# Experts from the seventh on in an order counted on chip, the two fullest with two blocks on one set of panels

## The chip, the cores and the metric

The kernel runs on one core of a Trainium2 chip. The metric is the device time of one execution in microseconds; smaller is better. It is one program: a first transformer block, a second block's mixer, and a mixture of experts (MoE) at the end. The change touches the MoE alone, the last 330 us or so.

## The reference, cut to what matters

```python
T = 512; D_MODEL = 1024; N_EXPERTS = 32; TOP_K = 2; D_EXPERT = 256

def hierarchical_moe(h, w_group, b_group, w_router, b_router, w_gate, w_up, w_down):
    ...
    grp = jnp.argmax(grp_probs, axis=-1)              # one of 4 groups of 8 experts
    top_p, top_e = lax.top_k(jax.nn.softmax(in_grp, axis=-1), TOP_K)
    weights = p_grp[:, None] * top_p / jnp.sum(top_p, axis=-1, keepdims=True)
    expert_id = grp[:, None] * EXPERTS_PER_GROUP + top_e
    ...
    def run_block(args):
        xb, e, wb = args
        a = jax.nn.silu(xb @ w_gate[e]) * (xb @ w_up[e])
        return (a @ w_down[e]) * wb[:, None]
    ...
    y = jnp.zeros((T, D), h.dtype).at[slot_tok].add(out.reshape(cap, D))

# second_block, after its mixer:
#     x = x + gate2 * hierarchical_moe(modulate(rms_norm(x)), ...);  return rms_norm(x, final_norm_g)
```

All is float32. Each of 512 tokens goes to two experts, 1024 assignments in all. An expert has three weight panels (gate, up, down) of 1024 x 256 floats, 1.05 MB each. Routing is a function of the inputs: counted from the reference, the experts 0 to 31 get

25 7 19 47 22 11 27 40 | 8 80 59 5 32 11 29 34 | 16 32 40 34 14 35 30 15 | 55 89 56 43 12 41 48 8

tokens. Two of them are over 64: expert 9 with 80 and expert 25 with 89.

## The kernel before, in words

A unit of MoE work is a `Pair` (a job): two blocks of up to CAP = 64 tokens, side by side on the 128 partitions. Each block is multiplied with its own expert's panels, as two matmuls that each fill 64 columns of the array (`both`, L1887). Pair c holds experts 2c and 2c+1. Tokens past the 64th of an expert go to a seventeenth job, number NP = 16, whose two blocks (SX = 2) belong to whichever experts overflow; its six panels come by indirect DMAs on GpSimd (L1680) through a table `xi`. `ORDER` (L31) puts that job thirteenth. If there were more than SX such blocks, a conditional part (L1407) would run eight further jobs and the final norm again.

The loop over jobs (L1372) does for job i: transpose the activations `a` of job i-1 (`turn_a`: PE L212, ACT copy `aT` L1910); transpose the gathered tokens of job i+1 (`turn`, L1877); start the gather of job i+2 from `h2d` in DRAM (L1865, POOL queue); gate and up products (`up`: 32 matmul calls, 64 rows in the profile since a float32 matmul runs in two passes; then Silu L1900 on ACT and the scaling L1901 on DVE); and the down product of job i-1 (`product`, 16 rows), scaled on DVE (L1919) into `o`. A scheduler then orders the instructions on each engine, so `down` may come before or after the next `up`.

The result of a job goes one of two ways:

- **Scattered**: `o` is written by an indirect DMA to `ye` in DRAM (L1933), one row of 4 KB for each valid token. Near the end `results` (L1471) clears a tile, gathers the two rows of each token from `ye` (L1476), and DVE adds them to `x` (L1392).
- **Hot**: `o` is split into two float32r halves `k` (L198) and spread onto `x` by one-hot matmuls (`spread`, L1956, 8 steps of two, each step with one DVE addition L1964 that frees its PSUM bank). `HOT` lists eight pairs. In order of execution these are jobs 4, 6, 8, 10 and 13 to 16; the spreads of the last two belong in part to `tail`.

Panels land in 17 places that are used in turn (`place`, L1663). SP issues one DMA for each panel (L1676), in order, and before each it waits until PE is done with the panel 17 places earlier. Panels of job 0 start while the second block's last products run. The router (`route`, L1479) counts each token's position within its expert by matmuls, builds the table of gathers `tab` and of scatters `to`, and leaves the rest of the tables and the weights `ws` to `rest` (L1583), which DVE computes while job 0 starts.

Of the kernel before, what the change touches and what calls it, by code (L numbers as in the profile page):

```python
# [9 lines left out]
F32 = mybir.dt.float32  # L10
# [8 lines left out]
P = 128  # L19
# [41 lines left out]
def shape_constants():  # L61
# [27 lines left out]
        it(8) * P + i[:, None] - float(2 * T), np.broadcast_to(np.repeat([float(c not in HOT) for c in range(NP)], 2).astype(f), (P, 32)),  # L89
        it(NX), i[:, None] + 0.0 * it(1), (it(XT) + 1.0) * CAP,  # L90
# [8 lines left out]
class Emit:  # L99
# [1151 lines left out]
    def route_loads(self, mod, op):  # L1251
# [7 lines left out]
        widths = (4, 8, 32, P, 8, 32, NX, 1, XT)  # L1259
# [76 lines left out]
    def moe(self):  # L1336
# [3 lines left out]
        with ExitStack() as c0:  # L1340
# [3 lines left out]
            tab, to = (rp.tile([P, NP + NX // 2], I32, tag=n, name=n) for n in ("tab", "to"))  # L1344
            src = rp.tile([P, 2, 8], I32, tag="src", name="src")
# [133 lines left out]
    def route(self, r1, rp, tab, to, src, W, xb, nx, sc, kept, ws):  # L1479
        nc, I = self.nc, self.I  # L1480
        d4, d8, i32, iP, tokv, away, jx, ip, thr = self.rt
# [43 lines left out]
        m1 = first_max(ing, d8, 8, h12[:, 0])  # L1525
        ing2 = tl(NT, 8)
        V.scalar_tensor_tensor(ing2, h12[:, 0], -BIG, ing, op0=ALU.mult, op1=ALU.add)
        m2 = first_max(ing2, d8, 8, h12[:, 1])
# [36 lines left out]
        vm = tl(8, 32, dt=F32R)  # L1565
        tt_(vm, flat(E), bc(tokv, 32), ALU.mult)
# [6 lines left out]
        rows, last = table(vm, 32, slice(0, NP))  # L1573
# [4 lines left out]
        with self.tc.issue_after(last.ins):  # L1578
            V.tensor_copy(to[:, 0:NP], rows)
            V.tensor_copy(kept, tab[:, 0:NP])  # L1580
            V.tensor_copy(cum, b[:, 0:160])

        def rest(room, room2):  # L1583
            tl = carve(room)

            cnt = cum[:, 128:160]
            n5 = tl(32, XT)
            tt_(n5, bc(cnt, XT), row(thr, 32), ALU.is_gt)
            V.tensor_reduce(nx, n5, axis=AX.X, op=ALU.add)
            z = tl(32)  # L1590
            V.memset(z, 0.0)
# [3 lines left out]
            for o, v in ((ei, row(away, 8)), (xi, row(xb, 8))):  # L1595
                tt_(flat(t), flat(E), v, ALU.mult)
                V.tensor_reduce(o, flat(t), axis=AX.X, op=ALU.add)
# [3 lines left out]
            V.tensor_scalar(ov, pos, float(CAP), None, op0=ALU.is_ge)  # L1601
            V.scalar_tensor_tensor(c, bl, -float(CAP), pos, op0=ALU.mult, op1=ALU.add)

            tt_(xi, xi, bl, ALU.add)
            tt_(xi, xi, ov, ALU.mult)
            eq = tl(8, NX)
            tt_(eq, row(jx, 8), bc(xi, NX), ALU.subtract)
            V.tensor_scalar(eq, eq, -1.0, None, op0=ALU.is_equal)
            tt_(vx, eq, bc(tokv, NX), ALU.mult)
            tt_(oc, row(iC, 8), bc(c, CAP), ALU.is_equal)  # L1610
            rows, _ = table(vx, NX, slice(NP, None), "d")
            V.tensor_copy(to[:, NP:], rows)


            m, f = tl(8), tl(8)
            V.scalar_tensor_tensor(m, pos, float(CAP), ei, op0=ALU.is_lt, op1=ALU.mult)
            V.scalar_tensor_tensor(f, xi, SX + 0.5, ov, op0=ALU.is_le, op1=ALU.mult)
            tt_(m, m, f, ALU.add)
            tt_(f, ov, f, ALU.subtract)
            for i, v in enumerate((m, f)):  # L1620
# [3 lines left out]

            tl2 = carve(room2)
# [11 lines left out]

            ge, gs, ex, s1 = tl(NT, 4), tl(NT), tl(NT), tl(NT)
            tt_(ge, gl, bc(gm, 4), ALU.subtract)
            tt_(ex, m2, m1, ALU.subtract)  # L1640
            nc.scalar.activation(ge, ge, AF.Exp)
            nc.scalar.activation(ex, ex, AF.Exp)
            V.tensor_reduce(gs, ge, axis=AX.X, op=ALU.add)
            V.reciprocal(gs, gs)
            V.tensor_scalar(s1, ex, 1.0, None, op0=ALU.add)
            V.reciprocal(s1, s1)
            tt_(W[:, 0, :], gs, s1, ALU.mult)
            tt_(W[:, 1, :], W[:, 0, :], ex, ALU.mult)
# [21 lines left out]

    def panel_of(self, which, e):
# [3 lines left out]
        if e < 32:  # L1675
            nc.sync.dma_start(raw, w[e].rearrange("(p k) c -> p (k c)", p=P))  # L1676
        else:
            if e >= 32 + SX:
                nc.vector.memset(raw, 0.0)
# [6 lines left out]
def PANELS(c):  # L1686

    return [(w, 2 * c + s) for w in ("gate", "up") for s in range(2)] + [("down", 2 * c + s) for s in range(2)]
# [163 lines left out]
class Pair:  # L1852
# [50 lines left out]
    def turn_a(self):  # L1903
# [5 lines left out]
        self.aT = self.tl("aT", 2, P)  # L1909
# [11 lines left out]
    def down(self, kept=None):  # L1921
        em = self.em
        if kept is not None and self.c in HOT:
# [13 lines left out]
    def hot(self, kept):  # L1937
        em, nc = self.em, self.nc
        self.o = self.tl("o", D)
        if self.c in ORDER[-2:]:  # L1940
# [47 lines left out]
```

## Time and profile before

| | |
|---|---|
| median of 3 runs | 1559.29 us (1558.46 to 1559.35) |
| the profiled execution: its own time | 1565.86 us |
| span of its profile | 1564.1 us |
| PE busy, DVE, ACT, POOL | 1483.3 us (95%), 908.5 (58%), 581.0 (37%), 206.3 (13%) |
| bytes read from and written to HBM | 259.91 MB and 19.44 MB, 179 GB/s over the span |
| DMA rate in four of the last ten of 40 slices | 425, 425, 425 and 420 GB/s |

Time in the profile counts from the span's start. Matmuls are pipelined and their ends are modelled, so a busy PE is not PE at its peak; the distance between two starts tells more than one duration. The granted clock is TensorE's, 1.00 for 2.4 GHz and 0.50 for 1.2 GHz; a number between them is a mean over a stretch with some of each.

### The profile page before, as it was taken

To read this page: it belongs to the slowest core of one execution; us is meant where nothing else is said; L and a number is where in the kernel's file an instruction comes from. 1 tells how busy PE (TensorE), PEld (TensorE's weight loads), DVE (VectorE), ACT (ScalarE), POOL (GpSimd) and SP (SyncE) were. 2 spreads that over 40 slices of the span, in tenths; PEclk is the share of its full clock that TensorE was granted. 3 is DMA by queue.
4 is the path that set the end of the run, shared out by engine and by line. 5 is a ranking of instruction groups with operands and counts; after the bars stand their busy time and mean duration, and the time that the engine had idled before them with its cause. 6 is when DMAs were issued, how large, how long until landed. Compare 5 with 4: busy or idle time off the path is not lost.

```text
span 1564.1 us, 20461 instructions
## 1 busy us (share of the span) xinstructions
PE 1483.3 (95%) x7742; PEld 1159.7 (74%) x7742; DVE 908.5 (58%) x1934; ACT 581.0 (37%) x1227; POOL 206.3 (13%) x235
## 2 busy tenths in 40 slices
PE   7999899999999999999999999999999789998885
PEld 6877778787888888887888888888887655455542
DVE  5675787877676765468766352248855641433162
ACT  4444675743232323345444342236632211111012
POOL 2110131101011010030000010000022211012310
PEclk8999999999999999999999999999999989999998
DMA  5325103057656654333322333421167679999941
GB/s 187 106 65 181 65 28 95 1 155 261 204 163 214 201 176 135 123 135 100 118 82 54 96 113 124 141 94 55 39 224 286 258 313 401 425 425 425 420 192 56
DMA packets 133056, 271.09 MB, mean 173 GB/s; under 512 B 19237, under 2 KB 78662, under 8 KB 119897
## 3 DMA queue, kind: packets, MB, share of 16 engines
q1 hardware_dynamic: 119834, 241.87, 43.1%
q0 software_dynamic: 9664, 25.04, 4.3%
q10 hardware_dynamic: 3454, 2.82, 0.6%
q8 instruction: 63, 1.03, 0.3%
q14 instruction: 41, 0.33, 0.1%
HBM read 259.91 MB, written 19.44 MB: 179 GB/s over the span
## 4 chain that ended last, share of the span: by engine, by line
PE 66%; DMA 10%; DVE 6%; issue 5%; ACT 2%; POOL 2%; SPq 0%; ACTq 0%; DVEq 0%; POOLq 0%
PE b L152 18%; PE b L153 18%; PE b L151 18%; PE b L1887 4%; PE b L212 3%; DMA pw<-w_expert_gate 2%; DMA pw<-w_expert_down 2%; DMA pw<-w_expert_up 1%; DMA ye<-o,to 1%; DVE wl L145 1%; PE b L1956 1%; PE b L816 1%; DMA xg<-h2d,tab 1%; DMA pw<-ye,src 1%; PE b L817 1%
## 5 line engine op out<-in xcount | busy, mean ns | idle before, releaser
L145 DVE TENSOR_TENSOR wl<-wr,wh 128x512 fp32r<-128x512 f32 x349 | 237.4, 717 | 144.1 <-ACT wh L143 132.5
L143 ACT ACTIVATE wh<-wr 128x512 fp32r<-128x512 f32 x361 | 205.3, 622 | 305.8 <-PE b L152 146.6
L1887 PE MATMUL b<-pw,xT 128*64 128x256 f32 x1088 | 133.3, 385 | 1.5 <-DMA pw<-w_expert_gate,xi 1.5
L151 PE MATMUL b<-h2h,wh 128*128 128x512 f32 (+1 forms) x320 | 122.6, 384 | 0.0
L152 PE MATMUL b<-h2l,wh 128*128 128x512 f32 (+1 forms) x320 | 122.4, 383 | 0.0
L153 PE MATMUL b<-h2h,wl 128*128 128x512 f32 (+1 forms) x320 | 122.3, 382 | 0.0
L1887 PEld LDWEIGHTS b<-pw,xT 128*64 128x64 f32 x1088 | 82.9, 138 | 46.2 <-issue 10.6
L152 PE MATMUL b<-fl,wh 128*128 128x512 f32 (+1 forms) x288 | 105.3, 366 | 0.0
L151 PE MATMUL b<-fh,wh 128*128 128x512 f32 (+1 forms) x288 | 105.0, 367 | 0.2 <-ACT fh L197 0.2
L153 PE MATMUL b<-fh,wl 128*128 128x512 f32 (+1 forms) x288 | 105.2, 366 | 0.0
L152 PE MATMUL b<-wl,uh 128*128 128x512 f32 x256 | 99.9, 390 | 0.2 <-DVE wl L145 0.2
L151 PE MATMUL b<-wh,uh 128*128 128x512 f32 x256 | 100.1, 391 | 0.0
L153 PE MATMUL b<-wh,ul 128*128 128x512 f32 x256 | 99.8, 390 | 0.0
L492 DVE SCALAR_TENSOR_TENSOR acc<-wr,cond,acc 128x512 f32<-128x512 f32 x84 | 62.9, 749 | 38.7 <-DMA wr<-mod_w 37.0
L153 PEld LDWEIGHTS b<-h2h,wl 128*128 128x128 f32 x320 | 61.0, 190 | 11.5
L152 PEld LDWEIGHTS b<-h2l,wh 128*128 128x128 f32 x320 | 61.0, 190 | 11.3
L151 PEld LDWEIGHTS b<-h2h,wh 128*128 128x128 f32 x320 | 60.8, 191 | 11.3
L1887 PE MATMUL b<-pw,aT 128*64 128x512 f32 x272 | 67.5, 600 | 0.5 <-ACT aT L1910 0.5
L151 PEld LDWEIGHTS b<-fh,wh 128*128 128x128 f32 x288 | 54.1, 189 | 9.6 <-ACT fh L197 0.5
L152 PEld LDWEIGHTS b<-fl,wh 128*128 128x128 f32 x288 | 54.4, 189 | 8.9 <-DVE fl L198 0.2
L153 PEld LDWEIGHTS b<-fh,wl 128*128 128x128 f32 x288 | 54.4, 189 | 8.8
L151 PEld LDWEIGHTS b<-wh,uh 128*128 128x128 f32 x256 | 48.1, 188 | 11.1 <-issue 1.4
(586 smaller groups left out, 3288.9 us busy)
## 6 DMA issues: line engine op xcount, KB each, us to landing
wr<-w_in SPq DMA_DIRECT2D x33, 1024.0 KB
pw<-w_expert_gate SPq DMA_DIRECT2D x32, 1024.0 KB
pw<-w_expert_up SPq DMA_DIRECT2D x32, 1024.0 KB
pw<-w_expert_down SPq DMA_DIRECT2D x32, 1024.0 KB
wr<-mod_w SPq DMA_DIRECT2D x24, 1024.0 KB
wr<-w_up SPq DMA_DIRECT2D x16, 1024.0 KB
wr<-w_down SPq DMA_DIRECT2D x16, 1024.0 KB
wr<-w_cmp SPq DMA_DIRECT2D x4, 1024.0 KB
```

Of the source, the lines that this page charges most:

```text
L143: nc.scalar.activation(hi[:, c], raw[:, c], AF.Copy)
L145: (nc.gpsimd if i in pool else eng or nc.vector).tensor_tensor(lo[:, c], raw[:, c], hi.bitcast(F32)[:, c], op=ALU.subtract)
L151: mm(o, lh, rh, start=first, stop=False)
L152: mm(o, lh, rl, start=False, stop=False)
L153: mm(o, ll, rh, start=False, stop=last)
L212: self.nc.tensor.transpose(o, i, self.ident[:k, :k])
L492: nc.vector.scalar_tensor_tensor(acc, rv[:, k, :], self.cond[:, kk:kk + 1], acc, op0=ALU.mult, op1=ALU.add)
L816: nc.tensor.matmul(o, v, ph, start=kind == 2, stop=False)
L817: nc.tensor.matmul(o, v, pl, start=False, stop=kind == 1 and kb == qb)
L1887: self.nc.tensor.matmul(o[h, :], x[:, k, h], w[s](k), start=k == ks[0], stop=k == ks[-1])
L1956: self.nc.tensor.matmul(b, self.oh[:, tt * P:(tt + 1) * P], k[:, half * 512:half * 512 + 512], start=first and i == 0, stop=last and i == 1)
```

## The change

There are still 17 jobs. The first three are pairs 0 to 2 with experts 0 to 5 (SE = 6), as before. DVE then finds the two fullest of experts 6 to 31; they become jobs 3 and 4, and each has one set of three panels on which both of its blocks run (up to 128 tokens of one expert). The remaining 24 experts, in their old order, make jobs 5 to 16. Which expert that is, is data: DVE writes a list `eid`, SP loads an entry into a register (`expert`, L1705 of the changed kernel), and the DMA of a panel takes its address from the register. The overflow job is gone, and with it the six indirect panels; more than one extra block for a fullest expert, or any for another, leads to the conditional part. Hot are jobs 13 to 16 only; all others are scattered. The additions of gathered rows to `x` are pinned to the place that the program gives them. `aT` has one buffer instead of two.

```diff
-NP = 16
+SE = 6
+ND = 32 - SE
+NP = 17
+NB = 2 * NP
 NX = 16
-SX = 2
-HOT = (4, 6, 8, 10, 12, 13, 14, 15)
-ORDER = [*range(12), NP, *range(12, NP)]
+HOT = 13
...
+            self.eid = rp.tile([P, ND], I32, tag="eid", name="eid")
...
-                jobs = [Pair(self, ep, XG[i % XGS], tab, to, c) for i, c in enumerate(ORDER)]
+                jobs = [Pair(self, ep, XG[i % XGS], tab, to, i) for i in range(NP)]
...
-                hot = lambda i: i >= 0 and jobs[i].c in HOT
-                back = max(i for i in range(n) if not hot(i)) + 2
+                hot = lambda i: i >= HOT
+                back = HOT + 1
...
-                            nc.vector.tensor_tensor(x[:, tt, :], y[:, k, :], x[:, tt, :], op=ALU.add)
+                            self.pin(nc.vector.tensor_tensor(x[:, tt, :], y[:, k, :], x[:, tt, :], op=ALU.add))
...
-                with self.tc.If(more > SX):
-                    for c in range(NP + SX // 2, NP + NX // 2):
+                with self.tc.If(more > 0):
+                    for c in range(NP, NP + NX // 2):
...
-        rows, last = table(vm, 32, slice(0, NP))
+        rows, last = table(vm, SE, slice(0, SE // 2))
...
         def rest(room, room2):
...
+            V.scalar_tensor_tensor(key, cnt, 32.0, ko, op0=ALU.mult, op1=ALU.add)
+            V.tensor_reduce(m1, key, axis=AX.X, op=ALU.max)
+            V.tensor_scalar(o1, key, m1, None, op0=ALU.is_equal)
+            V.scalar_tensor_tensor(key, o1, -1e6, key, op0=ALU.mult, op1=ALU.add)
+            V.tensor_reduce(m2, key, axis=AX.X, op=ALU.max)
+            V.tensor_scalar(o2, key, m2, None, op0=ALU.is_equal)
...
+            V.tensor_copy(ids[:, 0:1], m1)
+            V.tensor_copy(ids[:, 1:2], m2)
+            V.tensor_copy(self.eid, ids)
...
+            rows, _ = table(vx, NB + NX - SE, slice(SE // 2, None), "d")
...
+    def expert(self, e):
+
+        return self.nc.values_load(self.eid[0:1, e - SE:e - SE + 1], engines=(mybir.EngineType.SP,), min_val=0, max_val=31,
+                                   skip_runtime_bounds_check_because="the numbers of the experts from SE to 31, by their counts")
+
     def panel_of(self, which, e):
...
-        if e < 32:
-            nc.sync.dma_start(raw, w[e].rearrange("(p k) c -> p (k c)", p=P))
+        if e < SE:
+            nc.sync.dma_start(raw, whole(w[e]))
+        elif e < 32:
+            nc.sync.dma_start(raw, whole(w[bass.ds(self.who[e], 1)].rearrange("o r c -> (o r) c")))
...
+def EXPERTS(c):
+    two = (SE // 2, SE // 2 + 1)
+    if c in two:
+        return [SE + two.index(c)]
+    return [2 * c + s - (2 if c > two[1] else 0) for s in range(2)]
...
         if self.panels is None:
+            em.who = {e: em.expert(e) for e in EXPERTS(self.c) if SE <= e < 32}
             self.panels = [em.panel_of(*w) for w in PANELS(self.c)]
+        if len(self.panels) == 3:
+            self.panels = [p for p in self.panels for _ in range(2)]
...
-        self.aT = self.tl("aT", 2, P)
+        self.aT = self.tl("aT", 2, P, bufs=1)
```

How the change moves instructions shows at three places. On SP, where the panels of job 2 end and those of job 3 begin (`pw` is a panel's place, `eid` the list of experts), there stood before:

```order
L1676 DMA pw_11180<-w_expert_down 128x2048
L1676 DMA pw_11182<-w_expert_down 128x2048
L1676 DMA pw_11258<-w_expert_gate 128x2048
L1676 DMA pw_11260<-w_expert_gate 128x2048
L1676 DMA pw_11262<-w_expert_up 128x2048
```

and now:

```order
L1716 DMA pw_11204<-w_expert_down 128x2048
L1716 DMA pw_11206<-w_expert_down 128x2048
L1707 TENSOR_LOAD eid
L1718 ISA
L1718 DMA pw_11285<-w_expert_gate 128x2048
L1718 ISA
L1718 DMA pw_11287<-w_expert_up 128x2048
L1718 ISA
L1718 DMA pw_11289<-w_expert_down 128x2048
L1707 TENSOR_LOAD eid
```

Job 3 has three panels for six, each expert has one load of its number, and each panel one more instruction (ISA, two multiplications of registers) ahead of its DMA.

On PE, in the middle of the MoE, before the change: from the end of the down product of job 8 (`aT`) to the gate product (`xT`) of job 9, with the first steps of a spread (`k`, `oh`).

```order
L1887 MATMUL b_11919<-pw_11744,aT_11836 64x512
L1887 MATMUL b_11919<-pw_11746,aT_11836 64x512
L1956 MATMUL b_11963<-k_11904,oh_11906 128x512
L1956 MATMUL b_11971<-k_11904,oh_11906 128x512
L1887 MATMUL b_11866<-pw_11854,xT_11720 64x256
L1956 MATMUL b_11963<-k_11905,oh_11906 128x512
L1956 MATMUL b_11971<-k_11905,oh_11906 128x512
L1956 MATMUL b_11979<-k_11904,oh_11906 128x512
L1956 MATMUL b_11979<-k_11905,oh_11906 128x512
```

In the changed kernel no row of a spread stands on PE before job 13's down product. 32 such rows are left ahead of the tail's, where there were 96.

On DVE, near the end, before the change: the split and the additions of gathered rows (L1392, `pw`), around the activations `a` of job 14.

```order
L1919 TENSOR_TENSOR o_12443<-b_12451,S_10015 128x512
L198 TENSOR_TENSOR k_12445<-o_12443,k_12444 128x512
L1392 TENSOR_TENSOR x_10012<-pw_12428,x_10012 128x1024
L1919 TENSOR_TENSOR o_12443<-b_12459,S_10015 128x512
L1392 TENSOR_TENSOR x_10012<-pw_12428,x_10012 128x1024
L198 TENSOR_TENSOR k_12445<-o_12443,k_12444 128x512
L1901 SCALAR_TENSOR_TENSOR a_12424<-b_12407,ws,a_12424 128x256
```

and now:

```order
L1972 TENSOR_TENSOR o_12349<-b_12357,S_10015 128x512
L1972 TENSOR_TENSOR o_12349<-b_12365,S_10015 128x512
L201 TENSOR_TENSOR k_12351<-o_12349,k_12350 128x512 x2
L1954 SCALAR_TENSOR_TENSOR a_12330<-b_12313,ws,a_12330 128x256
L1928 COPY xT_12378<-b_12385 128x512
L1395 TENSOR_TENSOR x_10012<-pw_12333,x_10012 128x1024 x2
L1395 TENSOR_TENSOR x_10012<-pw_12334,x_10012 128x1024
```

The first additions of gathered rows now stand behind job 13's `o` and `k` and behind job 14's `a`, where two of them stood ahead of these.

## Rows read from the trace of the kernel before

**Rows 1.** Stretches: busy of PE, PEld, DVE, ACT, POOL; granted clock, DMA share, GB/s.

```profile
1240.00:1260.00 20.00, 7.62 (x44) 5.87 (x42) 13.06 (x57) 0.57 (x3) 2.19 (x2) 0.67 1.00 410
1280.00:1300.00 20.00, 19.98 (x146) 11.06 (x142) 4.35 (x7) 1.88 (x5) 2.04 (x2) 1.00 0.98 394
...
1440.00:1460.00 20.00, 18.39 (x140) 11.34 (x142) 3.25 (x5) 2.68 (x6) 3.02 (x3) 1.00 1.01 423
1480.00:1500.00 20.00, 13.30 (x56) 6.27 (x54) 8.60 (x12) 2.55 (x5) 10.50 (x9) 0.83 0.97 387
1272.00:1500.00 228.00, 212.76 (x1408) 121.69 (x1406) 74.84 (x133) 26.89 (x56) 44.14 (x40) 0.99 1.00 414
```

**Rows 2.** ACT's timeline, the copies aT of jobs 3, 4, 5, 6, 7, 8.

```profile
1312.00 0.37 ACT L1910 COPY aT<-b 128x256 f32<-128x256 f32 x1 [6.99 <-PE b L212]
...
1324.16 0.37 ACT L1910 COPY aT<-b 128x256 f32<-128x256 f32 x1 [6.99 <-PE b L212]
...
1336.32 0.37 ACT L1910 COPY aT<-b 128x256 f32<-128x256 f32 x1 [0.79 <-PE b L212]
...
1355.56 0.37 ACT L1910 COPY aT<-b 128x256 f32<-128x256 f32 x1 [10.28 <-PE b L212]
...
1373.74 0.37 ACT L1910 COPY aT<-b 128x256 f32<-128x256 f32 x1 [7.89 <-PE b L212]
...
1386.66 0.37 ACT L1910 COPY aT<-b 128x256 f32<-128x256 f32 x1 [4.28 <-PE b L212]
```

**Rows 3.** The same timeline, aT of jobs 9 to 14, and of job 16.

```profile
1407.12 0.37 ACT L1910 COPY aT<-b 128x256 f32<-128x256 f32 x1 [7.20 <-PE b L212]
...
1420.04 0.37 ACT L1910 COPY aT<-b 128x256 f32<-128x256 f32 x1 [4.27 <-PE b L212]
...
1440.49 0.37 ACT L1910 COPY aT<-b 128x256 f32<-128x256 f32 x1 [7.20 <-PE b L212]
...
1455.24 0.37 ACT L1910 COPY aT<-b 128x256 f32<-128x256 f32 x1 [4.38 <-PE b L212]
...
1466.96 0.37 ACT L1910 COPY aT<-b 128x256 f32<-128x256 f32 x1 [6.99 <-PE b L212]
...
1490.26 0.37 ACT L1910 COPY aT<-b 128x256 f32<-128x256 f32 x1 [2.45 <-PE b L212]
...
1531.21 0.37 ACT L1910 COPY aT<-b 128x256 f32<-128x256 f32 x1 [7.87 <-PE b L212]
```

**Rows 4.** SP's timeline: the wait for the first free place, the last panels.

```profile
1270.66 4.28 SPq L1676 DMA_DIRECT2D pw<-w_expert_gate  x2
...
1497.74 1.17 SPq L1676 DMA_DIRECT2D pw<-w_expert_down  x2
```

**Rows 5.** What SP waited for in 1230 to 1565: us, times, longest.

```profile
SPq L1676 <- PE b L1887: 123.6, 20, 25.4
```

**Rows 6.** All on panels: least, median, most from issue to landing.

```profile
DMA to landing us min/median/max: 8.1/12.9/24.9
```

**Rows 7.** DVE's timeline: idle before job 0, and near the end.

```profile
1261.55 0.69 DVE L1878 COPY xT<-b 128x512 f32<-128x512 f32 x1 [4.76 <-PE b L212]
...
1484.36 1.22 DVE L1392 TENSOR_TENSOR x<-pw,x 128x1024 f32<-128x1024 f32 x1 [11.83 <-DMA pw<-ye,src]
```

**Rows 8.** DMA, 1180 to 1565: GpSimd's queue in all; its issues, median us to landing.

```profile
q0 software_dynamic: 5904, 15.00, 10.1%
...
ye<-o,to POOLq DMA_INDIRECT x9, 8.4
pw<-ye,src POOLq DMA_INDIRECT x8, 10.7
```

**Rows 9.** By line, 1250 to 1565: count; busy us, mean ns; idle before.

```profile
L1887 PE MATMUL b<-pw,xT 128*64 128x256 f32 x1088 | 133.3, 385 | 1.5 <-DMA pw<-w_expert_gate,xi 1.5
```

**Rows 10.** By line: ns least, median, most; first and last start.

```profile
L1405 SPq TENSOR_LOAD <-nxi x1: 776/776/776, 1553.8 to 1553.8; - x1
...
L1676 SPq DMA_DIRECT2D pw<-w_expert_gate x32: 327/330/971, 1175.0 to 1474.7; - x32
```

More of the change, by code (lines that the diff above doesn't have):

```diff
@@ L88, in shape_constants @@
         4.0 - it(4), 8.0 - it(8), it(32), it(P),
-        it(8) * P + i[:, None] - float(2 * T), np.broadcast_to(np.repeat([float(c not in HOT) for c in range(NP)], 2).astype(f), (P, 32)),
-        it(NX), i[:, None] + 0.0 * it(1), (it(XT) + 1.0) * CAP,
+        it(8) * P + i[:, None] - float(2 * T),
+        np.where(it(32) < SE, -1e6, 31.0 - it(32)), np.where(it(32) < SE, it(32), it(32) + 4.0),
+        it(NB + NX), i[:, None] + 0.0 * it(1), (it(XT) + 1.0) * CAP,
         (i[:, None] < i[None, :]).astype(f),
@@ L1542, in route @@
         cum = tl(160, pool=rp)
-        pos, ei, xi, bl, ov, c = (tl(8, pool=rp) for _ in range(6))
+        pos, xi, bl, ov, c = (tl(8, pool=rp) for _ in range(5))
         oq = self.xp.tile([P, D], F32R, tag="B2", name="oc")
-        oc, vx = (oq[:, a:a + 8 * w].rearrange("p (i c) -> p i c", i=8) for a, w in ((0, CAP), (8 * CAP, NX)))
+        oc, vx = (oq[:, a:a + 8 * w].rearrange("p (i c) -> p i c", i=8) for a, w in ((0, CAP), (8 * CAP, NB + NX - SE)))
         C = slice(0, CAP)
@@ L1578, in route @@
         with self.tc.issue_after(last.ins):
-            V.tensor_copy(to[:, 0:NP], rows)
-            V.tensor_copy(kept, tab[:, 0:NP])
+            V.tensor_copy(to[:, 0:SE // 2], rows)
             V.tensor_copy(cum, b[:, 0:160])
         def rest(room, room2):
-            tl = carve(room)
+            tl, tl2 = carve(room), carve(room2)
             cnt = cum[:, 128:160]
-            n5 = tl(32, XT)
+            key, o1, o2, one, run = (tl(32) for _ in range(5))
+            m1, m2, lo, hi = (tl(1) for _ in range(4))
@@ new lines, in rest @@
+            tt_(key, o2, i32, ALU.mult)
+            V.tensor_reduce(m2, key, axis=AX.X, op=ALU.add)
+            tt_(lo, m1, m2, ALU.min)
+            tt_(hi, m1, m2, ALU.max)
+            ids = tl(ND)
+            V.tensor_scalar(ids[:, 2:], i32[:, 0:ND - 2], float(SE), None, op0=ALU.add)
+            for v in (lo, hi):
+                V.scalar_tensor_tensor(ids[:, 2:], ids[:, 2:], v, ids[:, 2:], op0=ALU.is_ge, op1=ALU.add)
+            V.tensor_copy(ids[:, 0:1], m1)
+            V.tensor_copy(ids[:, 1:2], m2)
@@ new lines, in rest @@
+            V.tensor_copy(self.eid, ids)
+            z, base = tl(32), tl(32)
+            V.memset(z, 0.0)
+            tt_(one, o1, o2, ALU.add)
+            V.tensor_tensor_scan(out=run, data0=one, data1=z, initial=0.0, op0=ALU.add, op1=ALU.add)
+            tt_(base, bo, run, ALU.subtract)
+            tt_(run, base, one, ALU.mult)
+            tt_(base, base, run, ALU.subtract)
+            for o, v in ((o1, SE), (o2, SE + 2)):
+                V.scalar_tensor_tensor(base, o, float(v), base, op0=ALU.mult, op1=ALU.add)
@@ L1594, in rest @@
             t = tl(2, NT, 32)
-            for o, v in ((ei, row(away, 8)), (xi, row(xb, 8))):
-                tt_(flat(t), flat(E), v, ALU.mult)
+            nb, sg = tl(8), tl(8)
+            for o, v in ((nb, base), (sg, one), (xi, xb)):
+                tt_(flat(t), flat(E), row(v, 8), ALU.mult)
                 V.tensor_reduce(o, flat(t), axis=AX.X, op=ALU.add)
@@ L1610, in rest @@
-            tt_(oc, row(iC, 8), bc(c, CAP), ALU.is_equal)
[L1611 to L1620, printed above, removed]
+            tt_(xi, xi, sg, ALU.subtract)
@@ new lines, in rest @@
+            tt_(xi, xi, nb, ALU.subtract)
+            V.scalar_tensor_tensor(xi, xi, float(NB - 1), ov, op0=ALU.add, op1=ALU.mult)
+            tt_(nb, nb, bl, ALU.add)
+            tt_(nb, nb, xi, ALU.add)
+            eq = tl2(8, NB + NX)
+            tt_(eq, row(jb, 8), bc(nb, NB + NX), ALU.is_equal)
+            tt_(vx, eq[:, :, SE:], bc(tokv, NB + NX - SE), ALU.mult)
+            tt_(oc, row(iC, 8), bc(c, CAP), ALU.is_equal)
+            rows, _ = table(vx, NB + NX - SE, slice(SE // 2, None), "d")
@@ new lines, in rest @@
+            V.tensor_copy(to[:, SE // 2:], rows)
+            V.tensor_copy(kept, tab[:, 0:NP])
+            ge, gs, ex, s1 = tl(NT, 4), tl(NT), tl(NT), tl(NT)
+            tt_(ge, gl, bc(gm, 4), ALU.subtract)
+            tt_(ex, g2, g1, ALU.subtract)
+            nc.scalar.activation(ge, ge, AF.Exp)
+            nc.scalar.activation(ex, ex, AF.Exp)
+            V.tensor_reduce(gs, ge, axis=AX.X, op=ALU.add)
+            V.reciprocal(gs, gs)
+            V.tensor_scalar(s1, ex, 1.0, None, op0=ALU.add)
@@ new lines, in rest @@
+            V.reciprocal(s1, s1)
+            tt_(W[:, 0, :], gs, s1, ALU.mult)
+            tt_(W[:, 1, :], W[:, 0, :], ex, ALU.mult)
+            tt_(eq, eq, bc(W.rearrange("p k t -> p (k t)"), NB + NX), ALU.mult)
+            wb = self.bank("d")
+            for i in range(8):
+                nc.tensor.matmul(wb[:CAP, 0:NB + NX], oc[:, i, :].bitcast(F32), eq[:, i, :], start=i == 0, stop=i == 7)
+            beside(ws, wb[C, 0:NB + NX], V.tensor_copy)
+            m = tl(8)
+            V.tensor_scalar(m, nb, 2 * HOT - 0.5, None, op0=ALU.is_le)
@@ L1686, in PANELS @@
 def PANELS(c):
-    return [(w, 2 * c + s) for w in ("gate", "up") for s in range(2)] + [("down", 2 * c + s) for s in range(2)]
+    return [(w, e) for w in ("gate", "up", "down") for e in EXPERTS(c)]
+def EXPERTS(c):
[3 more added lines that the diff above has]
+    return [2 * c + s - (2 if c > two[1] else 0) for s in range(2)]
 class Parts:
@@ L1922, in down @@
         em = self.em
-        if kept is not None and self.c in HOT:
+        if HOT <= self.c < NP:
             self.hot(kept)
```

62 lines of the change are left out of this document (20 added, 42 removed).

## The prediction

> **What bounds the kernel now.** I read the stretches of the MoE first, then when each job's activations turn, then the queue of panels on SP, and last DVE and GpSimd near the end.
>
> Two things run close to their limits at once. From 1280 on the DMA engines are full: 394 and 423 GB/s in the stretches shown, 414 GB/s as the mean of 1272 to 1500 [rows 1]. PE is full too: 212.76 of those 228 us are busy. So neither alone tells what a saving is worth; both have to be followed to the end.
>
> PE's pace shows in the copies `aT`, one for each job. Without a spread they stand 12.16 us apart (1312.00 to 1324.16), or 12.92 us (1373.74 to 1386.66) where the down product comes ahead of the next gate product and PE waits for `a` [rows 2]. With a spread between them it is 19.24 us (to 1355.56), 18.18 (to 1373.74) [rows 2], 20.46 (1386.66 to 1407.12) and 20.45 (1420.04 to 1440.49) [rows 2, 3].
>
> The panels' pace is slower than a job without a spread: six panels of 1.049 MB and some 0.5 MB of gathered and scattered tokens, 6.8 MB at 423 GB/s [rows 1], take 16.1 us. What lets PE go at 12.2 us at first is a lead of 17 panels. SP then lives off freed places: 123.6 us of its waits are for PE, the longest 25.4 us for the first place, free at 1270.66 [rows 4, 5]. In flight a panel takes 12.9 us [rows 6].
>
> The end is on PE. The last panels are issued at 1497.74 [rows 4] and land about 8.1 us later [rows 6], near 1506; job 16's `aT` comes at 1531.21 [rows 3], 25 us behind. From there to the span's end at 1564.1 are 32.9 us of last products, spreads and norm, which the change leaves as they are.
>
> **What the change removes.**
>
> - *Four spreads* (64 of 96 rows). By the distances above: 19.24 - 12.16, 18.18 - 12.16, 20.46 - 12.92 and 20.45 - 12.92, 28.2 us of PE's path.
> - *The overflow job's indirect panels.* Job 12 took 14.75 us (1440.49 to 1455.24) [rows 3], 1.8 over 12.92, which I put down to these.
> - *The stall at the first gathered rows.* Job 14 took 23.3 us (1466.96 to 1490.26) [rows 3]. DVE stood 11.83 us for the rows from `ye` [rows 7], with job 13's `o` and the next activations queued behind; PE's stretch there has 13.30 busy of 20 us, at a clock of 0.83 [rows 1]. Against 12.92 and about 2 us for the final norm's broadcast that falls there, the stall is 8.4 us. In the new order job 13's `o` and `k` and job 14's `a` stand ahead of the wait. The last scatter that the rows need is job 12's. From its issue to landing 8.4 us, then a gather of 10.7 us [rows 8], with two or three more issues between: some 22 us, while at least one and a half jobs, 24 us at the panels' pace, pass until DVE comes to the additions. So I count the stall as gone, with a few us as its upper bound.
>
> PE's path alone would be 38.4 us shorter.
>
> - *Six panels of 102*, 6.29 MB. Against that, 13 jobs scatter where nine did: by the reference's counts 746 rows instead of 485, 4 KB each, written once and read once, 2.14 MB more. (The counts fit the 15.00 MB on GpSimd's queue [rows 8]: 6.29 of indirect panels, 4.19 of gathered tokens, 1.99 written, 1.99 read and 0.52 of one broadcast make 14.98.) Net 4.15 MB, 10.0 us at 414 GB/s.
>
> **When the panels end.** At 1270.66 the 17 places are full and 79 panels are left, 82.8 MB; with 3.8 MB of token gathers, 3.06 MB written and 3.06 read it is 92.7 MB. At 414 GB/s [rows 1] that is 224 us, so the last bytes come near 1495. The same sum for before (85 panels, 89.1 MB, with 3.8 and twice 1.99) gives 234 us and 1505, against 1506 by the rows above. So the transfers give 10 us.
>
> **How the two meet.** Without the spreads PE uses up its lead at 16.1 - 12.5 us a job. At job 5 the lead is about 22 us (its gate and up panels are the first 11 of the 79, near 1302 at 224 / 79 = 2.84 us each; PE comes to them at 1324 [rows 2]), so near job 11 PE begins to wait for panels, some 3 us a job. Of its 38 us it gives back what passes the transfers. At the end, job 16's gate panels are four ahead of the last, four times 2.5 us, near 1486. Then follow its gate and up products (133.3 / 17 = 7.8 us busy [rows 9]), a spread (7.5, as above) and a us of transposes: `aT` near 1502 to 1504, where it was 1531. Job 15 must be done with its own by 1486. Its panels land some 20 us before, enough for 7.8, a spread and the 4.4 that are left of 12.16 for the down product and the transposes, with nothing to spare. **I take 1504, 27 us earlier.**
>
> **What it adds.**
>
> - *SP:* 26 loads of a number. A load takes 0.776 us [rows 10], 20 us in all, two for a job. The Trainium skill has a floor for this load, about 0.6 us ("DMA: Bandwidth & Descriptors", section "Latency and other measured facts"): an estimate of 15.6 us in place of 20.2. The row decides here, and both stay off the path. The 78 register multiplications have no row: between 0 and the 0.776 us of a load; I take 0.1, since no memory is read. An issue with a constant address takes 0.33 us, at most 0.97 [rows 10]; between these I bound one with a register, and take 0.33, since queue and shape are the same. At the upper ends SP needs 2 x 0.78 + 6 x 1.75 = 12.1 us a job, at the lower 3.5, both under 16.1. What covers it are the panels in flight, five at 12.9 us against 2.5 us each; without that cover each job would pay its two loads, 1.6 us. I take 0 to 1 us at the end, where PE waits.
> - *The first number.* `eid` is ready on DVE soon after the copy at 1261.55 [rows 7]; SP waits for its first free place until 1270.66 anyway [rows 4]. Nothing, with 8 us of cover.
> - *DVE:* 82 instructions from the first table to `ws` where there were 72, most of them small. DVE sat idle for 4.76 us there [rows 7]. Nothing to 3 us; I take 0.5, since PE comes to the second table some 2 us later in the new order.
> - *One buffer for `aT`:* the copy waits for the previous down product, which PE has done before the transposes that the copy needs. Nothing, and no gain.
>
> Sum: 27 less 1 is **26 us**. The profiled execution took 1565.86 us, 6.6 over the median of 1559.29; the difference is taken from the median: **1533 us**.
>
> **The rivals.**
>
> - *The panels go slower (0.17).* Register addresses or the longer queue on SP keep the rate at 394 GB/s, the lowest full stretch [rows 1]: 92.7 MB take 235 us, 11 us more, so a gain of 15: 1544. For it: PE has no lead left at the end. Against: same size, shape and queue.
> - *The panels never bind (0.12).* At 423 GB/s the panels end 5 us earlier and PE keeps most of its 38.4: a gain of 34 to 38, 1521 to 1525.
> - *The clock falls (0.06).* PE that waits for panels again and again is granted less: 0.67 in 1240 to 1260, where it was idle for 12 us, and 0.83 in 1480 to 1500, but 1.00 in 1440 to 1460 with 1.6 us idle [rows 1]. If each of six late jobs lost as 1480 to 1500 did, 17% of 20 us or 3.4 us, it would give back 20: 1553. The Trainium skill says that an idle array drops to half clock and gets it back after sustained work ("TensorE: Matmul & The Clock Gate", section "Part 1: The HAM clock gate"); waits of 3 us a job lie nearer the row that kept 1.00.
> - *SP becomes the bound, slower than before (0.04).* If an issue with a register address, its multiplications and loads held SP for longer than a panel's share, 2.84 us, each us beyond costs 78 us. From 3.2 us on the change loses (26 us are 0.33 us on 78 panels); at 3.5 us it is 1533 + 51, 1584. Against: 0.33 and 0.776 us [rows 10].
> - *It doesn't do what it says (0.01).* A third expert over 64 tokens would start the conditional part: eight jobs of six panels, 8 x 16.1 = 129 us or more, 1662. The reference's counts rule it out.
>
> **Numbers.** The forecast has 0.60, with 1526 to 1540. The range of 1519 to 1551 takes in the slower panels and the free PE. About 0.2% (3 us) can be told from no change: faster 0.92 (the forecast, the two rivals after it and half of the falling clock), same 0.03, slower 0.05.
>
> **What would show it.** No spread before job 13 and copies `aT` 12 to 13 us apart up to job 9 or 10, then 15 to 17; DMA full until 1490 to 1497; the last `aT` near 1504; SP's loads near 0.8 us; no wait over 3 us at the first addition from `ye`. Wrong it is if PE waits for panels before job 8, if SP's issues take over 2 us, or if the last panels land after 1500.

## The result: 17 us faster, and the profile after

| | before | changed |
|---|---|---|
| median (4 runs each) | 1559.32 us (1558.46 to 1562.03) | 1542.14 us (1539.57 to 1544.28) |
| ratio, 95% interval | | 0.9882 (0.986 to 0.9903) |
| the profiled execution: its own time, span | 1565.86, 1564.1 us | 1541.89, 1540.0 us |

17 us were gained where 26 were forecast (1533; range 1519 to 1551). The two profiled executions differ by more, 24.1 us of span, because 4.9 us of it lie ahead of everything that the change touches. The router's last logit (the last addition to `LT` on DVE) stands 4.9 us earlier, which is chance: in four traces of the kernel before and of edits to its MoE it stands between 1233.5 and 1241.2. Here it is first in the trace of before, then of the changed kernel:

```profile
1241.22 0.25 DVE L1327 SCALAR_TENSOR_TENSOR LT<-b,ss,rb 128x36 f32<-128x36 f32 x1 [0.41 <-PE b L212]
```
```profile
1236.29 0.26 DVE L1330 SCALAR_TENSOR_TENSOR LT<-b,ss,rb 128x36 f32<-128x36 f32 x1 [0.41 <-PE b L215]
```

All stage times below are therefore counted from that row. From it to the span's end took 322.9 us and takes 303.7: 19.2 us less. "Turn" is the place of a job in the loop, 0 to 16.

**The copies aT**, ACT's timeline of the changed kernel, turns 6, 7 and 9 to 16 (before: [rows 2, 3]):

```profile
1344.32 0.37 ACT L1963 COPY aT<-b 128x256 f32<-128x256 f32 x1 [6.98 <-PE b L215]
...
1356.47 0.37 ACT L1963 COPY aT<-b 128x256 f32<-128x256 f32 x1 [6.96 <-PE b L215]
...
1382.29 0.37 ACT L1963 COPY aT<-b 128x256 f32<-128x256 f32 x1 [4.27 <-PE b L215]
...
1396.88 0.37 ACT L1963 COPY aT<-b 128x256 f32<-128x256 f32 x1 [5.94 <-PE b L215]
...
1416.01 0.37 ACT L1963 COPY aT<-b 128x256 f32<-128x256 f32 x1 [9.49 <-PE b L215]
...
1433.71 0.37 ACT L1963 COPY aT<-b 128x256 f32<-128x256 f32 x1 [9.05 <-PE b L215]
...
1447.96 0.37 ACT L1963 COPY aT<-b 128x256 f32<-128x256 f32 x1 [5.60 <-PE b L215]
...
1465.88 0.37 ACT L1963 COPY aT<-b 128x256 f32<-128x256 f32 x1 [4.28 <-PE b L215]
...
1486.82 0.37 ACT L1963 COPY aT<-b 128x256 f32<-128x256 f32 x1 [5.18 <-PE b L215]
...
1505.91 0.37 ACT L1963 COPY aT<-b 128x256 f32<-128x256 f32 x1 [9.98 <-PE b L215]
```

The spreads are gone and the copies stand 12.2 us apart to turn 7, and 12.9 in the next two. Then the panels bind: 14.6, 19.1, 17.7 and 14.2 us for turns 10 to 13. The last three gaps (17.9, 20.9, 19.1) are turns with spreads, where PE waits for no panel in this trace. The waits of PE in 1360 to 1500 (us, times, longest) say the same:

```profile
PE b L1937 <- DMA pw<-w_expert_up: 7.1, 4, 2.8
...
PE b L2009 <- DVE x L2017: 3.4, 4, 1.9
```

**The stretches** (the columns are those of [rows 1]):

```profile
1410.00:1420.00 10.00, 9.28 (x52) 5.15 (x50) 1.25 (x3) 0.96 (x2) 1.02 (x1) 0.83 1.01 429
1420.00:1430.00 10.00, 7.50 (x56) 5.13 (x54) 1.31 (x2) 0.38 (x1) 1.01 (x1) 0.89 1.01 420
...
1450.00:1460.00 10.00, 9.99 (x46) 4.56 (x45) 2.67 (x4) 2.32 (x4) 8.62 (x8) 0.83 1.01 423
...
1490.00:1500.00 10.00, 8.10 (x50) 4.39 (x47) 9.52 (x12) 1.65 (x3) 0.00 (x0) 1.00 0.29 120
```

DMA is full until 1489. What still comes behind that, up to 1500, would be done near 1493 at the full rate, 256.6 us behind the last logit. The clock is below 1.00 in the panel-bound stretch and shortly after it.

**SP** by line (ns least, median, most; first and last start): the loads of a number, the multiplications, and the issue with a register address, which answer to [rows 10].

```profile
L1707 SPq TENSOR_LOAD <-eid x26: 262/270/491, 1266.1 to 1464.3; - x26
```
```profile
L1718 SPq FUSED_REGOPS  x78: 37/37/51, 1266.7 to 1477.3; - x78
...
L1718 SPq DMA_DIRECT2D pw<-w_expert_gate x26: 332/333/646, 1266.9 to 1467.5; - x26
```

So 26 loads take 7 us, not 20, a multiplication 0.04 us, and an issue 0.33 as before.

**DVE at the first addition** of gathered rows; [rows 7] had 11.83 us of waiting here, and now there is none:

```profile
1467.66 3.61 DVE L1395 TENSOR_TENSOR x<-pw,x 128x1024 f32<-128x1024 f32 x3
```

### The profile page after: what moved, and what is told of

It is laid out like the page before. It is cut to its first block, busy times and chain, and to the rows that moved or that the text cites. A ratio compares the mean times of both kernels' runs of the same rounds, so it can differ in the third digit from the quotient of the medians.

```text
span 1540.0 us, 20461 instructions
## 1 busy us (share of the span) xinstructions
PE 1460.1 (95%) x7678; PEld 1146.2 (74%) x7678; DVE 883.8 (57%) x1903; ACT 575.5 (37%) x1219; POOL 204.2 (13%) x233
## 4 chain that ended last, share of the span: by engine, by line
PE 67%; DMA 13%; DVE 6%; ACT 2%; issue 1%; POOL 1%; SPq 0%; ACTq 0%; DVEq 0%; POOLq 0%
PE b L154 18%; PE b L155 18%; PE b L156 18%; PE b L1937 6%; DMA pw<-w_expert_gate 4%; DMA pw<-w_expert_down 3%; PE b L215 3%; DMA pw<-w_expert_up 3%; DMA gm<-gd 1%; DVE wl L148 1%; PE b L819 1%; DMA xg<-h2d,tab 1%; PE b L820 1%; PE b L762 1%; DMA wr<-w_up 1%
## 5 line engine op out<-in xcount | busy, mean ns | idle before, releaser
L1954 DVE SCALAR_TENSOR_TENSOR a<-b,ws,a 128x256 f32<-128x256 f32 x17 | 8.2, 483 | 106.5 <-PE b L1937 106.5
```

Of the source, the lines that this page charges most:

```text
L1954: nc.vector.scalar_tensor_tensor(self.a, gu[1], em.ws[:, self.c:self.c + 1], self.a, op0=ALU.mult, op1=ALU.mult)
```

## The experiments

All times from the last logit, read as above from each run's profile; the ratio is to the kernel before on the same chip.

| run | aT of turn 13 | from the first aT to it | aT of turn 16 | end | median, ratio (95%) |
|---|---|---|---|---|---|
| before | 225.7 | 191.0 | 290.0 | 322.9 | 1559.3 |
| changed | 211.7 | 175.7 | 269.6 | 303.7 | 1542.1, 0.9882 (0.986 to 0.9903) |
| e5 changed again | 210.5 | 175.8 | 270.2 | 304.7 | 1543.1, 0.989 (0.9868 to 0.9912) |
| e1 fixed addresses | 207.6 | 172.9 | 265.5 | 299.6 | 1539.0, 0.987 (0.9853 to 0.9887) |
| e2 additions not pinned | 210.3 | 175.8 | 277.5 | 311.6 | 1549.4, 0.994 (0.992 to 0.996) |
| e3 no additions | 208.9 | 175.9 | 272.2 | 304.7 | 1542.7, 0.9899 (0.988 to 0.9917) |
| e4 a spare place | 208.9 | 173.5 | 274.1 | 306.5 | 1544.3, 0.9899 (0.9882 to 0.9915) |
| e6 six panels fewer | 194.1 | 161.2 | 250.6 | 285.3 | 1520.7, 0.975 (0.973 to 0.977) |
| e7 before, no early spreads | 221.4 | 186.5 | 286.0 | 318.9 | 1558.1, 0.9994 (0.9978 to 1.001) |
| e8 three spreads at the end | 211.5 | 176.5 | 276.4 | 309.0 | 1544.3, 0.9902 (0.9882 to 0.9923) |
| e9 before, six panels fewer | 221.8 | 188.9 | 293.8 | 328.2 | 1565.3, 1.0053 (1.0034 to 1.0072) |
| e10 before, neither | 205.6 | 172.4 | 279.0 | 312.9 | 1549.5, 0.9944 (0.9926 to 0.9962) |
| e11 broadcast early | 209.1 | 175.7 | 270.3 | 302.9 | 1543.5, 0.9912 (0.9889 to 0.9935) |
| e12 fullest spread early | 214.4 | 178.5 | 275.3 | 307.4 | 1544.8, 0.9925 (0.9898 to 0.9952) |

Not all of a row is its edit's doing. The first aT stands at 36.0 in the changed kernel, at 34.7 in e5 and at 33.0 in e3, which are one program up to there. What differs is the clock that PE was granted 20 to 30 us behind the last logit, first in the changed kernel, then in e3:

```profile
1256.29:1266.29 10.00, 9.35 (x52) 5.54 (x52) 6.81 (x28) 2.54 (x4) 0.99 (x1) 0.62 0.14 47
```
```profile
1256.32:1266.32 10.00, 9.57 (x88) 6.59 (x89) 8.29 (x36) 2.25 (x3) 1.02 (x2) 0.89 0.41 136
```

From there to turn 13 the changed kernel, e5, e2 and e3 agree to 0.2 us (175.7 to 175.9). So what an edit does up to turn 13 is read from the third column (differences are taken before rounding).

### What the four spreads and the six panels are worth: e7, e9, e10

```diff
-                    j.up(jobs[i - 2].spread(x) if hot(i - 2) else ())
+                    j.up(jobs[i - 2].spread(x) if i - 2 >= 13 and hot(i - 2) else ())
```
```diff
-            self.panels = [em.panel_of(*w) for w in PANELS(self.c)]
+            self.panels = em.last if self.c == NP else [em.panel_of(*w) for w in PANELS(self.c)]
+        em.last = self.panels
```

e7 has the first edit, e9 the second, e10 both, all on the kernel before. (The spreads left out are four; "five" in the two texts is a slip, the 64 products are right.)

> The kernel before, with the spreads of its five busy jobs ahead of job 13 left out (64 of the 96 products with k and the additions of their results to x; the jobs' order, panels, scatters and gathers stay). Theory A (the spreads are the change's whole gain, and panels take back the rest): 15 to 20 us faster than before, the copies aT 12 to 13 us apart up to job 8 or 9 and 15 or more behind it. Theory E: all 28 us. Theory G (the gain needs the fewer bytes and the quiet first gathered rows as well): 10 or less.

**No change at all**: 0.9994. Every theory on record allowed some gain; G comes nearest. PE did go ahead, until it ran out of panels. The waits of PE for panels in 1330 to 1470 of e7, and the last logit and turn 13's aT there:

```profile
PE b L1887 <- DMA pw<-w_expert_up: 9.1, 5, 4.0
...
PE b L1887 <- DMA pw<-w_expert_gate: 3.7, 3, 1.6
```
```profile
1237.78 0.25 DVE L1327 SCALAR_TENSOR_TENSOR LT<-b,ss,rb 128x36 f32<-128x36 f32 x1 [0.41 <-PE b L212]
```
```profile
1459.13 0.37 ACT L1910 COPY aT<-b 128x256 f32<-128x256 f32 x1 [7.00 <-PE b L212]
```

In the kernel before the same stretch has one wait for a panel, 1.5 us. Of 28 us of PE's work only 4.5 are left at turn 13 (186.5 for 191.0 from the first aT), and the medians show none of it.

> The kernel before, with the six indirect panels of its overflow job left out (its products use the panels of job 11); all spreads stay. 6.29 MB less to move. Theory P (up to job 12 PE's own work and the panels are level, so that either saving alone meets the other): 0 to 4 us faster than before, and DMA no longer full all the way. Theory Q (the panels alone set the time): 15 to 22 us faster.

> The kernel before without the five early spreads and without the six indirect panels. Theory P: far more than the sum of the two alone (0 for the spreads, 0 to 4 for the panels): 18 to 24 us faster than before, copies aT 12 to 13 us apart up to job 11. Theory Q: as without the six panels, within 2 us.

At turn 13 theory P holds: from the first aT the spreads alone give 4.5 us, the panels alone 2.1, **both together 18.5**. The last logit and turn 13's aT of e9, then of e10:

```profile
1234.80 0.26 DVE L1327 SCALAR_TENSOR_TENSOR LT<-b,ss,rb 128x36 f32<-128x36 f32 x1 [0.41 <-PE b L212]
```
```profile
1456.64 0.37 ACT L1911 COPY aT<-b 128x256 f32<-128x256 f32 x1 [6.99 <-PE b L212]
```
```profile
1233.47 0.25 DVE L1327 SCALAR_TENSOR_TENSOR LT<-b,ss,rb 128x36 f32<-128x36 f32 x1 [0.41 <-PE b L212]
```
```profile
1439.04 0.37 ACT L1911 COPY aT<-b 128x256 f32<-128x256 f32 x1 [7.46 <-PE b L212]
```

By the end e10 keeps only 10 us, and e9 is slower than before, which nobody expected. Both lose it in turn 14, at the first gathered rows: 31.8 us (e9) and 33.7 us (e10) from aT to aT, where the kernel before takes 23.3. PE's wait there in e9 (1456 to 1492):

```profile
PE b L1957 <- DVE x L1965: 12.9, 1, 12.9
```

The rows need the last scatter, DVE waits for the rows, and PE waits for DVE to add the spread's results to `x`. (In e10 DVE's longest wait there is 9.8 us, for the rows; in e9 it is 10.7 us, which the profile puts down to POOL's clearing of places, issued behind the first gathers.) In the kernel before PE's longest wait there is 6.3 us, for the copy `gf` that ACT does behind job 13's `k`. Part of the difference is the scheduler's: in e9 it put five of the spread's products between job 14's gate and up products, where the kernel before has three behind them. How much that is, no run tells apart; the two are compared at turn 13, ahead of it.

### The stall at the gathered rows: e2, e3

```diff
-                            self.pin(nc.vector.tensor_tensor(x[:, tt, :], y[:, k, :], x[:, tt, :], op=ALU.add))
+                            nc.vector.tensor_tensor(x[:, tt, :], y[:, k, :], x[:, tt, :], op=ALU.add)
```

> The changed kernel without the pins on the sixteen additions of gathered rows, so that the scheduler may place them: DVE then comes to the first of them ahead of job 14's last activation, and would wait there. Theory A: the rows land near 1468, job 14's activation is due at 1464.7 and waits behind the additions, 5 to 8 us slower, and PE's clock falls in that stall. Theory C (until the panels have landed, PE has slack there): within 1 us.

1549.4, 7 us slower, as theory A had it. DVE's waits for the rows in 1440 to 1490, and what PE then waited between job 14's products:

```profile
DVE x L1395 <- DMA pw<-ye,src: 7.3, 4, 2.2
```
```profile
1459.96 0.80 PE L2009 MATMUL b<-k,oh 128*128 128x512 f32 x1 [5.04 <-DVE x L2017]
```

Turn 14 takes 28.9 us instead of 17.9. So without the pin, one word of the diff, the change loses 11 us in turn 14, as e10 loses 10 there against the kernel before, and with its additions free it stands at 0.994, like e10.

In e3 the call is replaced by `pass`.

> The changed kernel with the additions of the gathered rows to x left out (the rows are still gathered), 16 DVE operations of 1.2 us. Theory A: PE waited 3.4 us for DVE's x in the spreads after 1467, so 2 to 4 us faster. Theory D (what is missing of the forecast is the rest of the stall at the gathered rows): 6 to 9 us faster. Theory C: within 1 us.

Theory C: 0.9899, no change that can be told. PE's waits for `x` behind turn 13 fell from 3.4 to 0.6 us, but the scheduler moved the spread's products forward into turn 14, which took 23.9 us with a mean clock of 0.86.

### Register addresses and lead: e1, e4

```diff
-        return self.nc.values_load(self.eid[0:1, e - SE:e - SE + 1], ...
+        return [25, 9, 6, 7, 8, *range(10, 25), *range(26, 32)][e - SE]
...
-            nc.sync.dma_start(raw, whole(w[bass.ds(self.who[e], 1)].rearrange("o r c -> (o r) c")))
+            nc.sync.dma_start(raw, whole(w[self.who[e]]))
```

> The changed kernel, with the experts' numbers as constants: the same panels in the same order, no loads of a number on SP and no multiplications of registers. Theory A (the panels bind PE between jobs 8 and 13, and register addresses cost nothing, since SP's loads of 0.27 us and issues of 0.33 us lie under the panels in flight): within 1 us of the changed kernel's 1542. Theory B (the missing part of the forecast gain, some 6 to 9 us, is what register addresses cost the panels): 1533 to 1536, with DMA over 430 GB/s between 1320 and 1480.

Theory B is out: 420 GB/s between 1320 and 1480 against 422. But A's "nothing" is not the whole of it. The median is 3 to 4 us lower; the intervals of the ratio overlap, so the time alone doesn't settle it. At turn 13 e1 is 2.8 us ahead, where the four traces of the changed order lie within 0.2 us. The trace shows a place for it, at the start. The 36 us from 8.25 us ahead of the first aT, of e1, the changed kernel and the kernel before:

```profile
1261.68:1297.68 36.00, 35.84 (x292) 22.13 (x290) 15.44 (x48) 4.04 (x9) 6.03 (x6) 1.00 0.92 353
```
```profile
1264.00:1300.00 36.00, 35.84 (x292) 22.13 (x290) 14.45 (x41) 4.02 (x9) 6.03 (x6) 1.00 0.83 320
```
```profile
1267.76:1303.76 36.00, 35.87 (x290) 22.01 (x288) 10.60 (x36) 4.02 (x9) 5.06 (x5) 1.00 0.90 349
```

And SP there, in the changed kernel, then in e1:

```profile
1271.08 0.33 SPq L1718 DMA_DIRECT2D pw<-w_expert_down  x1
1282.61 0.33 SPq L1718 DMA_DIRECT2D pw<-w_expert_gate  x1
```
```profile
1268.61 0.38 SPq L1717 DMA_DIRECT2D pw<-w_expert_down  x1
1273.41 0.33 SPq L1717 DMA_DIRECT2D pw<-w_expert_up  x1
1273.84 6.78 SPq L1717 DMA_DIRECT2D pw<-w_expert_gate  x2
```

With register addresses SP's panels stand in the order of the program: 11.5 us pass until the place of job 0's down panel comes free for job 4's gate panel. With constants the scheduler had put an up panel and a gate panel into this gap, 4.8 us behind the same down panel. 33 GB/s over 36 us are 1.2 MB, a little over one panel, and 2.8 us at 420 GB/s: what e1 is ahead at turn 13. So the price of a register address seems to be not its issue but the order that it fixes; e1 drops the loads and multiplications too, and no run keeps the order without them.

```diff
+                    if i == 0:
+                        last = I["w_expert_down_2"][0][EXPERTS(2)[1]].rearrange("(p k) c -> p k c", p=P)
+                        for k in range(2):
+                            self.pin(nc.scalar.dma_start(XG[2 + k], last[:, k]))
...
+            self.panels = [em.panel_of(*w) for w in names[:5]] + [em.spare] if self.c == 2 else [em.panel_of(*w) for w in names]
```

> The changed kernel with an eighteenth place, used once: the last down panel of job 2 goes into the two tiles xg2 and xg3 that stand empty until job 13, issued by ACT as two halves near 1261, where DMA moves little. One panel less has to be moved in the full stretch. Theory A: 2 to 4 us faster (2.5 us for a panel, and less time at the low clock). Theory E (PE's own work alone sets the end after the spreads are gone): within 1 us.

The gain was there and was lost again: turn 13's aT comes 2.2 us earlier, counted from the first aT, but turns 15 and 16 take 24.9 and 22.5 us instead of 20.9 and 19.1, with 4.1 us of waits for DVE's `x` and a clock of 0.86 in turn 15. By the time theory E's "within 1 us" can't be excluded, but not for its reason.

### The changed kernel again, and with less to move: e5, e6

> The changed kernel once more, unchanged, for its spread: 1539 to 1545 if the first four runs are typical. Of the trace: the time from the last logits LT to the end within 2 us of 303.7, copies aT 12.2 us apart up to job 7, and stretches at half clock behind PE's waits for panels in jobs 10 and 11, as in the first trace, though not at the same places.

As expected, 1543.1, with the same stretches of low clock (they lie in turns 11 and 12, one later than the text counts).

```diff
-            self.panels = [em.panel_of(*w) for w in PANELS(self.c)]
+            self.panels = em.last if self.c == 9 else [em.panel_of(*w) for w in PANELS(self.c)]
+        em.last = self.panels
```

> The changed kernel, with job 9's six panels left out: its products use those of job 8. 6.29 MB less to move, PE's work the same. Theory A (panels bind PE from job 8 to 13): the six panels are 15 us of transfers, PE's waits for panels (6.4 us between 1360 and 1460) and the half clock behind them (10 us at half speed, 5 lost) go, 8 to 12 us faster, with copies aT 12 to 13 us apart up to job 13. Theory E (PE's own work sets the end after the spreads are gone): within 1 us.

**22 us**, more than theory A's 12 and more than the 15 us that 6.29 MB take at 420 GB/s. PE's only wait for a panel in 1330 to 1470 is

```profile
PE b L1937 <- DMA pw<-w_expert_up: 0.3, 1, 0.3
```

and gaps are 12 to 14 us up to turn 13, which comes 14.5 us earlier, counted from the first aT. That is about the transfer time, and as PE hardly waits any more it is also about all that panels cost the changed kernel up to there. Turns 14 to 16 are 1.5 to 3.2 us shorter. The rest of the 20 us between the traces lies ahead of the first aT (32.9 for 36.0 and 34.7) and of the last logit, where the edit does nothing; what the medians have beyond that stays open.

### Attempts at a better version: e8, e11, e12

e11 loads the final norm's row in turn 1 by ACT into `xg2` and multiplies it out in turn 11; e8 has this and `HOT = 14`, with all gathers in turn 15 and half of the additions behind job 16's products; e12 has e11's edit and job 3 among the hot ones:

```diff
-HOT = 13
+HOT, FULL = 13, 3
...
-                hot = lambda i: i >= HOT
+                hot = lambda i: i >= HOT or i == FULL
```

> The changed kernel with job 13 scattered as the jobs before it (HOT 14), so that three spreads are left at the end, all four gathers in the loop's turn 15, half of their additions behind job 16's products, and the final norm's broadcast moved from the turn 15 to the turn 11, where PE waits for panels, from a row in xg2. Theory A: from job 13 on PE is the bound; without a spread (7.5 us), the broadcast (2.0) and the half clock behind it (1.8 lost) 7 to 11 us faster than the changed kernel. Theory H (the panels, 1 us later for 43 more rows scattered and gathered, set the pace to the end): 0 to 2 us.

> The changed kernel with the final norm's broadcast moved from the turn 15 to the turn 11, its row loaded by ACT into xg2; nothing else. Theory P (behind job 13 PE alone counts, ahead of it the panels): the two products of the broadcast (2.0 us) and the half clock behind them (1.8 lost) leave the end and fall where PE waits for panels anyway, and a place is free for one panel more: 3 to 5 us faster than the changed kernel, 1537 to 1540. Theory H (panels to the end): within 1 us.

> The broadcast moved as in the run before, and the job of the fullest expert (job 3) spread by PE instead of scattered and gathered: 89 rows of 4 KB less written and read, 0.73 MB, for 7 us of PE's work in turn 5, where PE is ahead of the panels. Theory P: the work is hidden, since PE waits 6 us and loses 5 to the half clock in jobs 9 to 12, and the bytes give 2 to 3 us beside the broadcast's 3 to 5: 1534 to 1538. Theory E (PE's own work sets the end): 7 us slower than the run before.

All three missed. e8 met the stall again: with one more job to scatter, turn 15 takes 32.0 us, and PE's waits in 1460 to 1500 are

```profile
PE b L2012 <- DVE x L2020: 9.7, 2, 7.3
```

e11 is ahead by 1.0 us at turn 14 (192.6 for 193.6 from the first aT) and 1.5 to 3.4 behind e5 and the changed kernel at turn 16: the scheduler put more of the last sums ahead of job 16's aT. In e12 turn 13 comes 2.8 us late, counted from the first aT, for 6.5 us of PE's early work, and its last panels are issued at 246.3 (244.5 in the changed kernel) though fewer bytes move: it may be that PE, being late, frees the places late; no run shows it alone. None beats the changed kernel.

## Why the prediction was right, and where it was short

- **Sign, mechanism and place were right.** Spreads gone, cadence 12.2 us, PE waits for panels from turn 10 on (1.1 us there, 3.2 in turn 11; forecast "near job 11"), DMA full to 1489, no wait at the first addition. None of the three signs of a wrong forecast came: no wait before job 8, issues of 0.33 us, the last panel issued at 1480.5 and the DMA traffic over by 1500. The size was not right: 1542 lies outside 1526 to 1540, which had 0.60, and inside the range by the room for slower panels. That job 16's aT stands at 1505.9, where the forecast said "near 1504", is luck: the whole trace stands 4.9 us earlier, and from the last logit it is 269.6 for 262.8.
- **The step that failed: "How the two meet".** It let PE meet the panels at the end, at job 16's gate panels (near 1486), with job 15 done by then "with nothing to spare". In truth PE meets them for the last time in turn 13 (in e5 and e11 in turn 14, for 1.0 and 1.1 us). Behind turn 13 lie 57.9 us (17.9 + 20.9 + 19.1) in which PE waits for no panel, but 3.4 us for DVE's `x`; e6, with six panels fewer, takes 56.4 for the same turns. Job 15's aT stands at 250.5 from the last logit, 5.7 us behind the 1486 that the step needed. At turn 13 the change gives 15.2 us, counted from the first aT (191.0 to 175.7; 14.0 from the last logit). The forecast's terms up to there, 28.2 and 1.8, less all that was to be given back to panels (38.4 less 27, 11.4), make 18.6. The order of the first panels, which the forecast did not see, is worth 2.8 of the 3.4 between them (e1). The transfers' sum itself was nearly right: 1495 was forecast, 253.8 us behind the last logit; it is 256.6.
- **The spreads were credited with 28.2 us that they don't have alone.** Their removal alone is worth nothing (e7), the six panels alone nothing or less (e9); at turn 13 the two together are worth 18.5. In the kernel before PE's work and panels were level there. The forecast's comparison of both saw this only as a lead that is used up.
- **The 2.14 MB more of scattered rows:** GpSimd's queue moved 10.84 MB, which fits 746 rows. Half of them, the rows gathered, are read behind turn 13 (first gather at 1449.55); the other half takes 2.5 us at 420 GB/s. At turn 13 the change stands 3.3 us behind e10, but e1, with the same rows, only 0.5. So the order of the panels accounts for most of it, and what the rows cost no run shows.
- **The stall** was put at 8.4 us and gives 5.4 (turn 14: 23.3 to 17.9). What holds it down is the pin (without it turn 14 takes 28.9, e2), which the prediction did not price apart from the new order.
- **"One more us" for SP and DVE** isn't shown: the first aT comes 1.2 us later (36.0 for 34.8), but in e5, the same program, it comes at 34.7. Loads take 0.27 us.
- **The falling clock** (0.06) came in part. Over 1410 to 1440 and 1450 to 1460 the clock of 0.83, 0.89, 0.94 and 0.83 is 5.1 us of full speed lost, where the rival said 20. The slower panels (0.17) named nearly the right time, mostly for a wrong reason: between 1320 and 1480 the rate did not fall (422 GB/s), but in the first 36 us it was 320 for 349 before, by the order of the panels if e1 is read rightly.

Sum at turn 16: 27 forecast, 20.4 measured. Of the difference 1.2 lie ahead of the first aT, 3.4 between it and turn 13, 3.0 at the stall, and 1.0 came back in the last two turns; the first and the last of these are no more than what e5 differs from the changed kernel (1.2 and 1.6). The tail behind is 1.2 us longer, which leaves 19.2 in the traces; the medians say 17.2.

## What to carry to other kernels

Where two resources are level, taking work from one is worth little, and the sum of two such edits says little of the two together: look for the last wait of the one for the other, price the change there, and price what lies behind it by itself. A register address that keeps a queue in program order can cost more than the instructions that it adds (here some 2.8 us, by e1). And an addition that waits for a transfer must be kept, in order, behind the work that could go ahead of it. Before two traces are compared, run the same program twice: where its own traces part, here ahead of the first aT, count from behind that point.

## What the runs showed of the hardware

**The clock falls behind a wait of 2.8 us, not in it.** One us each in the changed kernel: PE idle, PE busy at half clock (1.2 of 2.4 GHz), and back.

```profile
1408.00:1409.00 1.00, 0.00 (x0) 0.00 (x0) 0.00 (x0) 0.00 (x0) 0.00 (x0) 1.00 1.04 434
...
1411.00:1412.00 1.00, 1.00 (x6) 0.50 (x5) 0.00 (x0) 0.00 (x0) 0.00 (x0) 0.50 1.03 434
...
1415.00:1416.00 1.00, 0.58 (x5) 0.59 (x6) 0.36 (x1) 0.00 (x0) 0.00 (x0) 1.00 1.06 451
```

PE had stood from 1406.6 to 1409.4. The 30 rows of the up product behind it take 5.35 us, and 3.67 where the clock stays. The Trainium skill describes this for matmul loops that wait for DMA in each turn ("TensorE: Matmul & The Clock Gate", section "HAM oscillation — how this bites in real kernels"): the next tile starts at the low clock. The trace agrees in part: the half clock comes behind the waits of 2.79 and 2.50 us, but the product starts at the full clock and falls within 2 us, and the 1.7 us that this costs come on top of the wait.

Not settled: the low clock at 1455 to 1458 came with PE busy throughout, behind the final norm's products, whose operands fill one row. In e5, the same program, it didn't come; in e6 it came again, at 1437 to 1441, with PE busy before it.

**A load of a number** took 0.26 to 0.49 us, against 0.776 for the one in [rows 10]. The Trainium skill's floor of about 0.6 us ("DMA: Bandwidth & Descriptors", section "Latency and other measured facts") doesn't hold here.

Not tried: panels of jobs 3 to 5 in an order of the program that suits the places, which e1 suggests.
